# A mixer layer with a routed expert stage: one order for both sides of every condition, and last blocks of at most 64 rows with high and low parts side by side

## The chip, the cores and the metric

One core of a Trainium2 chip runs the whole kernel in one launch. The metric is the device time of one execution in microseconds (us), taken as the median of several executions. A profile is one further execution, recorded instruction by instruction.

## What is computed

One decoder layer on 2048 tokens of width 1024, in float32. First a mixer (an S5 state-space branch and a convolution branch, merged by gates, projected and normalised), then a mixture of 32 SwiGLU experts, of which each token uses two, then a second layer norm. The change touches the expert stage only; the reference of that stage, cut to what matters:

```python
zg = xt @ w_rg + b_rg                      # 4 groups: the best one is taken
ze = xt @ w_re + b_re                      # 8 experts a group: the best two of the group
gate = p_group * softmax(top_v)
eid = gsel * 8 + top_i                     # 4096 assignments of tokens to experts
# the tokens of an expert are put into blocks of ROW_BLOCK = 128 rows
def expert_block(args):
    idx, e = args
    xb = xt[idx]                                              # 128 x 1024
    hid = jax.nn.silu(xb @ w_gate[e]) * (xb @ w_up[e])        # 128 x 256
    return hid @ w_down[e]                                    # 128 x 1024
y = segment_sum(y_buf * w_buf[:, None], tok_buf, num_segments=n_tok)
```

How many rows an expert has is known only when the router has run. With the inputs of this case the counts of the 32 experts are 121, 75, 114, 74, 129, 25, 158, 106, 205, 200, 227, 36, 276, 286, 255, 177, 50, 58, 174, 160, 11, 119, 273, 99, 42, 54, 130, 211, 60, 77, 19 and 95. So 18 experts (called single here) have one block, 11 have two and 3 have three: 49 blocks. The last block has at most 64 rows in 18 experts: in nine single ones (5, 11, 16, 17, 20, 24, 25, 28 and 30) and in nine larger ones (4, 6, 12, 13, 15, 18, 19, 22 and 26).

## The kernel before

The mixer and the router take the span's first 1255 us or so; nothing of the change lies in them but a few small VectorE instructions of the router (`route2`), which turn a token's rank within its expert into a row of a table in HBM, `td`. The table says for each expert, block and partition which token stands there and with what weight. It is read back as `TAB` (`lists`).

**Arithmetic.** A product in full precision is made of three TensorE passes: each operand is split into a high part, rounded by ScalarE (ACT), and a low part, which VectorE (DVE) subtracts out; high x high, high x low and low x high are summed in PSUM. For an expert the weights are split as `egu` (gate and up, 8 pieces of 128 rows, four ACT copies and four DVE subtractions of 128x1024) and `edn` (down, two of each). A block's rows are split as `bh` and `bl` after they are transposed.

**A block.** `gateup` is 24 matmuls of 128x512 into `pg`; `act` makes `hid` from it (SiLU on ACT, a product on DVE); `turn` transposes the next block's gathered rows (eight into `pt`, from which ACT and DVE make `bh` and `bl`); `down` is 12 matmuls into `pd`, for the block before the present one, whose transposed `hid` is `hh` and `hl`; `turnh` transposes the present `hid` (two into `ph`). `emit` copies `pd` to `yy` on ACT, scaled by the rows' weights, and GpSimd (POOL) adds `yy` to the output rows in HBM by an indirect DMA, `acc`. TensorE's order is therefore `gateup`, `turn`, `down`, `turnh`, block after block. Whoever looks at a trace can take the first `ph` transpose as the mark between two blocks.

**Conditions.** The count is read into a register on each engine, and each engine branches for itself. `unit(e, b)` does a block and asks whether the expert has another; if so, it turns that block's rows and calls itself, if not, `over()` turns the next expert's rows. `JB = 4` blocks are written out for each expert, one within another, so that the ending `over()` stands four times in each expert's code, and the one of a single expert last: TensorE jumps there over three blocks and three endings, which are some 400 instructions with the weight loads. A two-block expert jumps over some 270. (An expert with more than 128 JB rows would get a loop at the end, which no expert of these inputs needs.)

**Weights.** While expert e is in its first block, `step` and `high`, `low` split the gate and up weights of expert e+1, whose raw bytes SP's queue loaded earlier, and then ask for those of e+3 (`load`); `high(1 - j, 4, 5)` and `low` do the same for `down`, once the old ones have been used.

Of the kernel before, what the change touches and what calls it, by code (L numbers as in the profile page):

```python
# [31 lines left out]
JB = 4  # L32
# [53 lines left out]
def layer(ctx, tc, a, out, dbg=None):  # L86
# [1102 lines left out]
    def route2(p, pk):  # L1189
# [7 lines left out]
        dv = oh[:, :, :, 0]  # L1197
        V.tensor_scalar(dv, rk, 1.0 / 128.0, -0.498, op0=OP.mult, op1=OP.add)
        V.scalar_tensor_tensor(rk, rk, 32.0, ef, op0=OP.mult, op1=OP.add)
        V.tensor_scalar(dv, dv, MAGIC, None, op0=OP.add)  # L1200
        V.tensor_scalar(dv, dv, MAGIC, -65535.0, op0=OP.subtract, op1=OP.mult)
        V.scalar_tensor_tensor(sl, rk, 16.0, dv, op0=OP.mult, op1=OP.add)
# [59 lines left out]
    for p in range(NP):  # L1262
# [47 lines left out]
        if p == NP - 3:  # L1310
# [30 lines left out]
    XA, XE = [[ep.tile([128, D], F32, name=f"{n}{i}") for i in range(2)] for n in ("xa", "xe")]  # L1341
    XC = [ep.tile([128, D], F32, name="xc0"),
          wp.tile([128, D], F32, name="xc1", tag="raw", bufs=1, padded_shape=[128, 1024])]
    zero = ident[:, 0:1].to_broadcast([128, D])
    for t in XA:
        A.activation(t, zero, AF.Copy, scale=0.0)
    high(0, 4, 5)
    for t in XE + XC:
        A.activation(t, zero, AF.Copy, scale=0.0)
    high(1, 0, 1)  # L1350

    def pairs(n, name, shape, dt=F32):
        return [ep.tile(shape, dt, name=f"{name}{i}") for i in range(n)]

    BH, BL = [[wp.tile([128, 8, 128], F32R, name=f"{nm}{i}", tag=tag, bufs=2) for i in range(2)]
              for nm, tag in (("bh", "hi"), ("bl", "lo"))]
    HH = pairs(2, "hh", [128, 2, 128], F32R)
    HL = pairs(2, "hl", [128, 2, 128], F32R)
    HID = pairs(2, "hid", [128, FF])
    TAB = ep.tile([128, NE, JB, 2], I32, name="tab")  # L1360
    IXL = pairs(3, "ixl", [128, 2], I32)
    IXQ = pairs(3, "ixq", [128, 2], I32)
# [3 lines left out]
    CNT, IX = {}, {}  # L1366

    def table(e):
        CNT[e] = nc.values_load(cnt[0:1, e:e + 1], engines=ENG, min_val=0, max_val=S)
        IX[e] = TAB[:, e]  # L1370
# [4 lines left out]
    def ends(e, b):  # L1375

        for t, r in ((IXL[e % 3], IX[e][:, b]), (IXQ[e % 3], IX[e][:, b - 1] if b else IXL[(e - 1) % 3])):
            V.tensor_copy(t[:, 0:1], r[:, 0:1])
            V.tensor_copy(t[:, 1:2].bitcast(F32), r[:, 1:2].bitcast(F32))
            if not e:  # L1380
                break
# [11 lines left out]
    def turn(xb, i):  # L1393
        for b in range(2):
            for k in range(4):
                PE.transpose(PT[b][:, k, :], xb[:, (4 * b + k) * 128:(4 * b + k + 1) * 128], ident)
            hi = BH[i][:, 4 * b:4 * b + 4, :]
            A.activation(hi, PT[b], AF.Copy)
            V.tensor_tensor(BL[i][:, 4 * b:4 * b + 4, :], PT[b], hi.bitcast(F32), op=OP.subtract)

    def gateup(i, gu):
        p, hi, lo = PG[i], BH[i], BL[i]
        for k in range(8):
            t = gu[k // 4]
            PE.matmul(p, hi[:, k, :], t[:, 0, k % 4, :], start=k == 0, stop=False)
            PE.matmul(p, hi[:, k, :], t[:, 1, k % 4, :], start=False, stop=False)
            PE.matmul(p, lo[:, k, :], t[:, 0, k % 4, :], start=False, stop=k == 7)

    def act(i, j):
        A.activation(HID[j], PG[i][:, 0:FF], AF.Silu)  # L1410
        V.tensor_tensor(HID[j], HID[j], PG[i][:, FF:2 * FF], op=OP.mult)

    def turnh(j):
        for k in range(2):
            PE.transpose(PH[:, k, :], HID[j][:, 128 * k:128 * k + 128], ident)
        A.activation(HH[j], PH, AF.Copy)  # L1416
        V.tensor_tensor(HL[j], PH, HH[j].bitcast(F32), op=OP.subtract)

    def down(j):
        hh, hl, dn = HH[j], HL[j], DN[j]  # L1420
        for h in range(2):
            c = slice(512 * h, 512 * h + 512)
            for k in range(2):
                PE.matmul(PD[h], hh[:, k, :], dn[:, 0, k, c], start=k == 0, stop=False)
                PE.matmul(PD[h], hh[:, k, :], dn[:, 1, k, c], start=False, stop=False)
                PE.matmul(PD[h], hl[:, k, :], dn[:, 0, k, c], start=False, stop=k == 1)

    def emit(ixc):
        y = ep.tile([128, D], F32, name="yy", bufs=2)
        for h in range(2):  # L1430
            A.activation(y[:, 512 * h:512 * h + 512], PD[h], AF.Copy, scale=ixc[:, 1:2].bitcast(F32))
        G.indirect_dma_start(out=acc, out_offset=bass.IndirectOffsetOnAxis(ap=ixc[:, 0:1], axis=0),
                             in_=y, in_offset=None, bounds_check=S - 1, oob_is_err=False, compute_op=OP.add)

    def unit(e, b):

        i, j = (e + b) % 2, e % 2
        gateup(i, GU[j])
        more = b == 0 and 0 < e < NE - 1
        if more:  # L1440
            step(1 - j, 0, 1, 2)
            high(1 - j, 3)
        if b == 1 and JB > 3:
            with tc.If(CNT[e] > 384):
                gather(XE[j], IX[e][:, 3, 0:1])
# [5 lines left out]
        jp, ixp = (j, IX[e][:, b - 1, :]) if b else (1 - j, None)  # L1451
# [10 lines left out]
        if b + 1 == JB:  # L1462
            over()
            return
        with tc.If(CNT[e] > 128 * (b + 1)) as c:
            turn((XE[j], XC[j], XE[j])[b], 1 - i)
            if e or b:
                down(jp)
                emit(ixp if b else IXL[(e - 1) % 3])
            turnh(j)  # L1470
            unit(e, b + 1)
        with c.Else():
            over()

    def extra(e):
        with tc.If(CNT[e] > 128):
            gather(XE[e % 2], IX[e][:, 1, 0:1])
            with tc.If(CNT[e] > 256):
                gather(XC[e % 2], IX[e][:, 2, 0:1])

# [4 lines left out]
    lists(2, NE - 2)  # L1485
    high(1, 2, 3, 4, 5)
    low(1, *range(6))
    for e in range(3):
        table(e)
    load(3, 1)  # L1490
    load2(3, 1)
    gather(XA[0], IX[0][:, 0, 0:1])
    gather(XA[1], IX[1][:, 0, 0:1])
    extra(0)
    turn(XA[0], 0)
    for e in range(NE):
        j = e % 2
        if e + 3 < NE:
            table(e + 3)
        if e + 2 < NE:  # L1500
            gather(XA[j], IX[e + 2][:, 0, 0:1])
        if e + 1 < NE:
            extra(e + 1)
        unit(e, 0)
        ahead_ = 0 < e < NE - 1
        if ahead_:
            high(1 - j, 4, 5)
            low(1 - j, 4)
        turnh(j)
        if ahead_:  # L1510
            low(1 - j, 5)
            if e + 3 < NE:
                load2(e + 3, 1 - j)
        if e:
            emit(IXQ[e % 3])
    down((NE - 1) % 2)
    emit(IXL[(NE - 1) % 3])
# [7 lines left out]
    with tc.If(mx > 128 * JB):  # L1525
        with tc.For_i(0, NE, 1) as e:
            c = nc.values_load(cnt[0:1, ds(e, 1)], engines=ALL, min_val=0, max_val=S)
            with tc.If(c > 128 * JB):
# [3 lines left out]
                with tc.For_i(JB, S // 128, 1) as b:  # L1532
                    with tc.If(c > b * 128):
# [3 lines left out]
                        gather(XA[0], ix[:, 0:1])  # L1537
                        turn(XA[0], 0)
                        gateup(0, GU[0])
                        act(0, 0)  # L1540
                        turnh(0)
                        down(0)
                        emit(ix)
# [133 lines left out]
```

## Time and profile before

| | us |
|---|---|
| median of 3 runs | 1860.15 (1859.89 to 1860.32) |
| the profiled execution | 1859.71 |
| its span, first to last instruction | 1857.6 |
| expert stage, first to last `ph` transpose of a block | 1285.97 to 1780.03 |

The profiled execution is 0.44 us below the median of the runs, and its time is 2.1 us more than its span. TensorE is busy for most of the span, in the mixer by nearly unbroken matmuls; in the expert stage all of TensorE, ACT, DVE and the DMA queues have work in each block, and which of them ends last differs from block to block. The granted clock of TensorE is given as a share of full speed.

### The profile page before, as it was taken

The page shows a single profiled execution, that of the slowest core. Times are in us where ns is not written, and L with a number is a line of the kernel's source. Part 1 is how long each engine was busy: PE and PEld are TensorE (multiplying, and loading weights), DVE is VectorE, ACT ScalarE, POOL GpSimd, SP SyncE. Part 2 cuts the span into 40 slices and gives each one's busy share as a digit, 9 for nine tenths or more (in the row PEclk, how much of TensorE's full clock was granted, in tenths as well). Part 3 has the DMA queues.
Part 4 walks back from the last instruction along what each step waited for, and adds up shares of the span by engine and source line. Part 5 has one row for each costly group of instructions (what it writes and reads, how often), then busy time and mean ns, then how long its engine had stood idle before and what let it go on. Part 6 is the DMA issues. An engine that isn't in the chain of part 4 may idle for free. (4 is left out here: it accounts for less than half of the span.)

```text
span 1857.6 us, 24068 instructions
## 1 busy us (share of the span) xinstructions
PE 1712.9 (92%) x8360; PEld 1376.4 (74%) x8361; DVE 1321.3 (71%) x2528; ACT 692.6 (37%) x1069; POOL 301.1 (16%) x318
## 2 busy tenths in 40 slices
PE   8999999999999999999999999974899998999940
PEld 7888877777777777877888888853677787877730
DVE  5798787687877884765576678885665556657748
ACT  5111222222222223533321122235665556657744
POOL 2000001101110110000000012212333332323215
PEclk9999999999999999999999999987999999999975
DMA  6321432432342336433553323456888878789755
GB/s 217 92 91 47 121 75 76 141 97 84 97 144 79 97 98 222 121 108 110 185 184 118 143 91 125 171 190 211 266 264 256 269 204 265 220 251 322 231 176 232
DMA packets 213924, 301.40 MB, mean 162 GB/s; under 512 B 29246, under 2 KB 159376, under 8 KB 211168
## 3 DMA queue, kind: packets, MB, share of 16 engines
q1 hardware_dynamic: 166496, 213.32, 35.4%
q0 software_dynamic: 23008, 56.06, 10.9%
q10 hardware_dynamic: 24224, 29.50, 4.7%
q8 instruction: 112, 1.84, 0.4%
q14 instruction: 84, 0.69, 0.1%
HBM read 224.28 MB, written 92.31 MB: 170 GB/s over the span
## 5 line engine op out<-in xcount | busy, mean ns | idle before, releaser
L66 PE MATMUL mm<-xh,whi 128*128 128x512 f32 x896 | 360.8, 403 | 0.0
L66 PE MATMUL mm<-xl,whi 128*128 128x512 f32 x896 | 353.5, 395 | 0.0
L66 PE MATMUL mm<-xh,wlo 128*128 128x512 f32 x896 | 352.2, 393 | 0.0
L66 DVE SCALAR_TENSOR_TENSOR cvw<-cvw,cw 128x1024 f32<-128x1024 f32 x240 | 292.1, 1280 | 0.0
L66 PE MATMUL pg<-egu,bh 128*128 128x512 f32 x784 | 251.5, 402 | 4.7 <-ACT hh L1416 2.8
L66 PEld LDWEIGHTS mm<-xh,whi 128*128 128x128 f32 x896 | 168.3, 188 | 47.9 <-ACT y L712 5.8
L66 PEld LDWEIGHTS mm<-xh,wlo 128*128 128x128 f32 x896 | 168.2, 188 | 41.4
L66 PEld LDWEIGHTS mm<-xl,whi 128*128 128x128 f32 x896 | 168.6, 188 | 36.4 <-issue 0.2
L66 DVE TENSOR_TENSOR egu<-eraw,egu 128x1024 fp32r<-128x1024 f32 x128 | 150.8, 1220 | 33.9 <-ACT egu L1245 33.9
L66 PEld LDWEIGHTS pg<-egu,bh 128*128 128x128 f32 x784 | 145.3, 190 | 37.6 <-ACT hh L1416 3.3
L66 PE MATMUL mm<-yt,whi 128*128 128x512 f32 x512 | 163.8, 401 | 2.0 <-ACT yt L858 1.5
L66 PE MATMUL mm<-wo,mh 128*128 128x512 f32 x512 | 163.6, 401 | 0.0
L66 PE MATMUL pg<-egu,bl 128*128 128x512 f32 x392 | 156.1, 398 | 1.1 <-DVE bl L66 1.1
L731 ACT ACTIVATE gt<-mm,cols 128x512 f32<-128x512 f32 x64 | 44.0, 687 | 265.5 <-PE mm L66 265.5
L66 PE MATMUL pd<-edn,hh 128*128 128x512 f32 x392 | 131.3, 416 | 11.3 <-issue 9.4
L1245 ACT ACTIVATE egu<-eraw 128x1024 fp32r<-128x1024 f32 x128 | 124.9, 1058 | 0.2 <-issue 0.2
L66 PEld LDWEIGHTS mm<-yt,whi 128*128 128x128 f32 x512 | 96.7, 190 | 26.0 <-ACT yt L858 1.5
L66 PEld LDWEIGHTS mm<-wo,mh 128*128 128x128 f32 x512 | 95.0, 190 | 21.8 <-issue 1.2
L66 DVE TENSOR_TENSOR edn<-erd,edn 128x1024 fp32r<-128x1024 f32 x64 | 77.9, 1219 | 38.8 <-ACT edn L1245 38.6
L66 PE MATMUL mm<-yt,wlo 128*128 128x512 f32 x256 | 101.7, 397 | 0.0
L66 PE MATMUL mm<-wo,ml 128*128 128x512 f32 x256 | 101.7, 397 | 0.0
L66 PEld LDWEIGHTS pd<-edn,hh 128*128 128x128 f32 x392 | 72.5, 195 | 27.4 <-issue 11.4
(287 smaller groups left out, 2646.3 us busy)
## 6 DMA issues: line engine op xcount, KB each, us to landing
eraw<-in_w_gate_dram SPq DMA_DIRECT2D x64, 512.0 KB
eraw<-in_w_up_dram SPq DMA_DIRECT2D x64, 512.0 KB
erd<-in_w_down_dram SPq DMA_DIRECT2D x32, 1024.0 KB
gd<-gt ACTq DMA_DIRECT2D x64, 256.0 KB
gl<-gd SPq DMA_DIRECT2D x64, 256.0 KB
wraw<-in_w_in_dram SPq DMA_DIRECT2D x28, 512.0 KB
xt<-in_x_dram SPq DMA_DIRECT2D x16, 512.0 KB
rg<-in_x_dram SPq DMA_DIRECT2D x8, 1024.0 KB
```

The source lines that it names most:

```text
L66: return f(*args, **kw)
L731: A.activation(gt, p, AF.Sigmoid, bias=cols[:, BI + 12 + m:BI + 13 + m])
L1245: A.activation(h, src, AF.Copy)
```

## The change

- `JB` is 3. The table `td` is laid out so that rows of a last block of at most 64 can also be read as 64 partitions (`TB2`): three more DVE instructions in each `route2`.
- `select()` works out for all experts at once, before the first block, which rows come next (`NX`) and which row list and weights a last block has (`LL`, `LQ`): some 27 small DVE instructions, and some 17 for masks ahead of it. The four small copies that `ends()` made for each expert are gone.
- `unit` and `over` give way to `block` and `further`. Both sides of the question whether there is another block end with `turnh()` alone; `turn` and `down` of the next expert stand ahead of the question, so they aren't copied. Some 272 instructions of TensorE are now jumped over by a single expert, some 137 by a two-block one.
- Each block asks whether it has more than 64 rows. If not, `gateup_small` uses `BE` as the stationary matrix: the 64 columns of the high part beside the 64 of the low part (every second column of each), so that 16 matmuls instead of 24 do; the result for the high part lies in PSUM's partitions 0 to 63, for the low part in 64 to 127. `act_small` copies the lower half out (`T`, ACT, 64x512), adds the upper half (DVE), and goes on with 64 rows.
- `B`, `HH`, `HL` and `HID` have one buffer each instead of two. The scale and the addition of an expert's last block (`emit`) come behind `turnh` of the next expert, ahead of the splitting of `edn`.

The diff, cut to its core:

```diff
-JB = 4
+JB = 3
...
-    def unit(e, b):
-
-        i, j = (e + b) % 2, e % 2
-        gateup(i, GU[j])
...
-        def over():
-            ends(e, b)
-            if e + 1 < NE:
-                turn(XA[1 - j], 1 - j)
-            if e or b:
-                down(jp)
-            if b and not e:
-                emit(ixp)
...
-        with tc.If(CNT[e] > 128 * (b + 1)) as c:
-            turn((XE[j], XC[j], XE[j])[b], 1 - i)
-            if e or b:
-                down(jp)
-                emit(ixp if b else IXL[(e - 1) % 3])
-            turnh(j)
-            unit(e, b + 1)
-        with c.Else():
-            over()
...
+    BE = B.rearrange("p k q (r t) -> p k (q r) t", t=2)[:, :, :, 0]
...
+    def gateup_small(i, gu):
+
+        p = PG[i]
+        for k in range(8):
+            t = gu[k // 4]
+            for q in range(2):
+                PE.matmul(p, BE[:, k], t[:, q, k % 4, :], start=k == 0 and q == 0, stop=k == 7 and q == 1)
+
+    def act_small(i):
+        A.activation(T, PG[i][64:128], AF.Copy)
+        V.tensor_tensor(T, T, PG[i][0:64], op=OP.add)
+        A.activation(HID[0:64], T[:, 0:FF], AF.Silu)
+        V.tensor_tensor(HID[0:64], HID[0:64], T[:, FF:2 * FF], op=OP.mult)
...
+    def block(e, b, i, gu):
+
+        with tc.If(CNT[e] > 128 * b + 64) as c:
+            gateup(i, gu)
+            act(i)
+        with c.Else():
+            gateup_small(i, gu)
+            act_small(i)
+
+    def further(e, b):
+
+        j = e % 2
+        with tc.If(CNT[e] > 128 * b) as c:
...
+            turnh()
+            block(e, b, (e + b) % 2, GU[j])
+            if e + 1 < NE or b + 1 < JB:
+                turn(XB[b])
+            down(j)
...
+        with c.Else():
+            turnh()
...
+    for e in range(NE):
+        j = e % 2
+        more = 0 < e < NE - 1
...
         if more:
             step(1 - j, 0, 1, 2)
             high(1 - j, 3)
-        act(i, j)
+        block(e, 0, j, GU[j])
         if more:
             low(1 - j, 3)
...
+        turn(XN[j])
+        if e:
+            down(1 - j)
+        further(e, 1)
+        if e:
+            emit(LQ[:, e, 0:1], LQ[:, e, 1:2])
+        if more:
             high(1 - j, 4, 5)
-            low(1 - j, 4)
-        turnh(j)
+            low(1 - j, 4, 5)
...
```

**ACT, at the change from one expert to the next.** Before, the splitting of the down weights stands ahead of the copy of the turned `hid`:

```order
L1245 ACTIVATE edn_10194<-erd 128x1024 x2
L1416 ACTIVATE hh_10166<-ph 128x256
L1431 ACTIVATE yy<-pd_10181,ixq_10177 128x512
L1431 ACTIVATE yy<-pd_10182,ixq_10177 128x512
L1369 TENSOR_LOAD cnt
L1476 COMPARE_AND_BRANCH
L1478 COMPARE_AND_BRANCH
L1478 UNCONDITIONAL_BRANCH x2
L1476 UNCONDITIONAL_BRANCH
L1245 ACTIVATE egu_9529<-eraw_9327 128x1024 x2
L1245 ACTIVATE egu_9995<-eraw_9327 128x1024 x2
L1410 ACTIVATE hid_10171<-pg_10180 128x256
```

In the changed program the same place of ACT reads:

```order
L1488 ACTIVATE hh<-ph 128x256
L1522 UNCONDITIONAL_BRANCH
L1503 ACTIVATE yy<-pd_10219,lq 128x512
L1503 ACTIVATE yy<-pd_10220,lq 128x512
L1249 ACTIVATE edn_10173<-erd 128x1024 x2
L1439 TENSOR_LOAD cnt
L1564 COMPARE_AND_BRANCH
L1567 COMPARE_AND_BRANCH
L1567 UNCONDITIONAL_BRANCH x2
L1564 UNCONDITIONAL_BRANCH
L1249 ACTIVATE egu_10179<-eraw_9816 128x1024 x2
L1249 ACTIVATE egu_10233<-eraw_9816 128x1024 x2
```

The two copies of `edn` have moved from ahead of `hh` to behind the two `yy`.

**DVE, in an expert's first block.** Before, DVE goes from the weights to `hid` and `bl` in this order (behind the branch are the rows of an expert with a further block):

```order
L66 TENSOR_TENSOR egu_9529<-eraw_9327,egu_9529 128x1024 x2
L66 TENSOR_TENSOR egu_9995<-eraw_9327,egu_9995 128x1024
L66 TENSOR_TENSOR hid_10171<-hid_10171,pg_10180 128x256
L66 TENSOR_TENSOR egu_9995<-eraw_9327,egu_9995 128x1024
L1465 COMPARE_AND_BRANCH
L66 TENSOR_TENSOR bl_10164<-pt_10183,bh_10162 128x512
L66 TENSOR_TENSOR bl_10164<-pt_10184,bh_10162 128x512
```

In the changed program there are two ways through the question on 64 rows:

```order
L66 TENSOR_TENSOR egu_9544<-eraw_9339,egu_9544 128x1024 x2
L66 TENSOR_TENSOR egu_10013<-eraw_9339,egu_10013 128x1024
L1512 COMPARE_AND_BRANCH
L66 TENSOR_TENSOR hid<-hid,pg_10218 128x256
L1512 UNCONDITIONAL_BRANCH
L66 TENSOR_TENSOR tt<-tt,pg_10218 64x512
L66 TENSOR_TENSOR hid<-hid,tt 64x256
L1512 UNCONDITIONAL_BRANCH
L66 TENSOR_TENSOR egu_10013<-eraw_9339,egu_10013 128x1024
```

The addition `tt` of a small block stands behind three subtractions of the next expert's weights, as `hid` does, and the fourth subtraction is still ahead of the low part of the rows.

**TensorE, in an expert's first block.** The changed program has the gate and up products twice, of which one is run:

```order
L66 MATMUL pg_10217<-egu_9544,bhl 128x512 x12
L66 MATMUL pg_10217<-egu_10013,bhl 128x512 x12
L1512 UNCONDITIONAL_BRANCH
L66 MATMUL pg_10217<-egu_9544,bhl 128x512 x8
L66 MATMUL pg_10217<-egu_10013,bhl 128x512 x8
L1512 UNCONDITIONAL_BRANCH
L66 MATMUL pt_10221<-ident,xhi 128x128 x4
```

Before, the end of that block, at the question whether there is another, was this:

```order
L66 MATMUL pg_10180<-egu_10191,bh_10163 128x512 x2
L66 MATMUL pg_10180<-egu_10191,bl_10165 128x512
L1465 COMPARE_AND_BRANCH
L66 MATMUL pt_10183<-ident,xe_10147 128x128 x4
L66 MATMUL pt_10184<-ident,xe_10147 128x128 x4
L66 MATMUL pd_10181<-edn_10152,hh_10166 128x512 x2
```

The `pt` rows now follow the products on every way; before, they stood on each side of the branch `L1465`, and a single expert's stood behind all others.

## Rows read from the trace of the kernel before

**Rows 1.** Windows: length, busy (instructions) of PE, PEld, DVE, ACT, POOL; clock; DMA.
```profile
1500.00:1550.00 50.00, 50.00 (x247) 41.09 (x246) 26.39 (x47) 27.75 (x45) 13.22 (x8) 1.00 0.75 209
```

**Rows 2.** Groups by line, PE, 1280 to 1790: busy, mean, idle before, releaser.
```profile
L66 PE MATMUL pg<-egu,bh 128*128 128x512 f32 x781 | 250.0, 401 | 4.7 <-ACT hh L1416 2.8 <-ACT edn L1245 1.7
L66 PE MATMUL pd<-edn,hh 128*128 128x512 f32 x392 | 131.3, 416 | 11.3 <-issue 9.4 <-ACT yy L1431 1.9
L66 PE MATMUL pt<-ident,xa 128*128 128x128 f32 x248 | 32.9, 275 | 9.4 <-issue 8.9 <-DMA xa<-hd,tab 0.5
L66 PE MATMUL ph<-ident,hid 128*128 128x128 f32 x98 | 19.0, 276 | 1.6 <-DVE ixl L66 1.4
```

**Rows 3.** Timeline of PE: start, length, instruction; expert 23's block, and the ends.
```profile
1285.97 0.41 PE L66 MATMUL ph<-ident,hid 128*128 128x128 f32 x2
...
1668.76 0.38 PE L66 MATMUL ph<-ident,hid 128*128 128x128 f32 x2
...
1669.44 0.39 PE L66 MATMUL pg<-egu,bl 128*128 128x512 f32 x1
...
1674.55 1.03 PE L66 MATMUL pt<-ident,xa 128*128 128x128 f32 x8
1675.34 0.72 PE L66 MATMUL pd<-edn,hh 128*128 128x512 f32 x2
...
1678.23 0.38 PE L66 MATMUL ph<-ident,hid 128*128 128x128 f32 x2
...
1780.03 0.38 PE L66 MATMUL ph<-ident,hid 128*128 128x128 f32 x2
```

**Rows 4.** Waits of PE for nothing shown, 1280 to 1790: total us, times, longest.
```profile
PE pd L66 <- issue: 9.8, 5, 4.7
PE pt L66 <- issue: 8.9, 7, 2.8
```

**Rows 5.** Timeline of PE, first waits behind the jumps of experts 3 and 17.
```profile
1315.18 1.07 PE L66 MATMUL pt<-ident,xa 128*128 128x128 f32 x8 [2.52 <-issue]
...
1573.27 1.22 PE L66 MATMUL pd<-edn,hh 128*128 128x512 f32 x2 [4.74 <-issue]
```

**Rows 6.** Windows, as rows 1, the six microseconds at that wait.
```profile
1572.00:1578.00 6.00, 4.73 (x15) 3.78 (x16) 1.59 (x7) 0.87 (x1) 0.00 (x0) 0.72 1.06 357
```

**Rows 7.** Timeline of ACT, expert 23's block.
```profile
1668.26 2.01 ACT L1245 ACTIVATE edn<-erd 128x1024 fp32r<-128x1024 f32 x2 [1.41 <-PE pd L66]
1670.17 0.36 ACT L1416 ACTIVATE hh<-ph 128x256 fp32r<-128x256 f32 x1
1670.43 1.25 ACT L1431 ACTIVATE yy<-pd,ixq 128x512 f32<-128x512 f32 x2
1671.58 3.90 ACT L1245 ACTIVATE egu<-eraw 128x1024 fp32r<-128x1024 f32 x4
```

**Rows 8.** Timeline of DVE, expert 23's block.
```profile
1672.67 3.50 DVE L66 TENSOR_TENSOR egu<-eraw,egu 128x1024 fp32r<-128x1024 f32 x3 [0.55 <-ACT egu L1245]
1676.08 0.41 DVE L66 TENSOR_TENSOR hid<-hid,pg 128x256 f32<-128x256 f32 x1
1676.41 1.22 DVE L66 TENSOR_TENSOR egu<-eraw,egu 128x1024 fp32r<-128x1024 f32 x1
1677.55 0.21 DVE L66 COPY ixl<-tab 128x1 int32<-128x1 int32 x2
1677.79 1.28 DVE L66 TENSOR_TENSOR bl<-pt,bh 128x512 fp32r<-128x512 f32 x2
```

**Rows 9.** Waits, 1280 to 1790: total us, times, longest.
```profile
ACT yy L1431 <- DMA acc<-yy,ixq: 13.7, 9, 2.8
```

**Rows 10.** Timelines of POOL, PE and DVE at the first block.
```profile
1268.21 1.90 POOL L1384 DMA_INDIRECT xa<-hd,tab  x1 [7.28 <-ACT egu L1245]
...
1276.33 1.94 PE L66 MATMUL pt<-ident,xa 128*128 128x128 f32 x8 [21.68 <-DMA xa<-hd,tab]
...
1278.08 0.69 DVE L66 TENSOR_TENSOR bl<-pt,bh 128x512 fp32r<-128x512 f32 x1 [6.64 <-ACT bh L1398]
```

More of the change, by code (lines that the diff above doesn't have):

```diff
@@ L1340, in layer, with rowt @@
     ep = ex.enter_context(tc.tile_pool(name="ep", bufs=1, side="right"))
-    XA, XE = [[ep.tile([128, D], F32, name=f"{n}{i}") for i in range(2)] for n in ("xa", "xe")]
-    XC = [ep.tile([128, D], F32, name="xc0"),
-          wp.tile([128, D], F32, name="xc1", tag="raw", bufs=1, padded_shape=[128, 1024])]
+    def rowt(tag):
+        return wp.tile([128, D], F32, name=f"x{tag}", tag=tag, bufs=2, padded_shape=[128, 1024])
+    X1, X2 = rowt("hi"), rowt("lo")
+    XN = [rowt("hi"), rowt("lo")]
@@ L1344, in layer @@
+    XB = [None, X1, X2]
     zero = ident[:, 0:1].to_broadcast([128, D])
-    for t in XA:
-        A.activation(t, zero, AF.Copy, scale=0.0)
+    A.activation(X1, zero, AF.Copy, scale=0.0)
     high(0, 4, 5)
-    for t in XE + XC:
+    for t in XN + [X2]:
         A.activation(t, zero, AF.Copy, scale=0.0)
     high(1, 0, 1)
[L1352 to L1356, printed above, removed]
@@ L1364, in layer @@
+    NX = ep.tile([128, NE, JB], I32, name="nx")
+    LP = ep.tile([128, NE, JB, 2], F32, name="lp")
+    LL = ep.tile([128, NE, 2], I32, name="ll")
+    LQ = ep.tile([128, NE, 2], I32, name="lq")
     ENG = [ET.PE, ET.Activation, ET.DVE, ET.Pool]
     ALL = ENG + [ET.SP]
-    CNT, IX = {}, {}
+    CNT = {}
+    for b in range(JB):
+        V.tensor_scalar(MK[:, :, b], pc, 128.0 * b, None, op0=OP.is_gt)
+    V.memset(MK[:, :, 0:1], 1.0)
+    V.tensor_tensor(OH[:, :, 0:JB - 1], MK[:, :, 0:JB - 1], MK[:, :, 1:JB], op=OP.subtract)
@@ L1368, in table @@
     def table(e):
         CNT[e] = nc.values_load(cnt[0:1, e:e + 1], engines=ENG, min_val=0, max_val=S)
-        IX[e] = TAB[:, e]
-    def lists(e, n):
-        A.dma_start(TAB[:, e:e + n].rearrange("p e b c -> p e (b c)"), dap(td, 32 * e, [[1024, 128], [32, n], [1, 2 * JB]]))
[L1375 to L1381, printed above, removed]
@@ L1403, in gateup @@
         for k in range(8):
             t = gu[k // 4]
[L1405 to L1413, printed above, removed]
+            PE.matmul(p, B[:, k, 0], t[:, 0, k % 4, :], start=k == 0, stop=False)
@@ new lines, in layer @@
+    low(0, 4, 5)
+    load2(2, 0)
+    lists(0, 2)
+    lists(2, NE - 2)
+    A.dma_start(TB2.rearrange("p e b c -> p e (b c)"), dap(td, 0, [[2048, 64], [32, NE], [1, 2 * JB]]))
+    gather(X1, TAB[:, 0, 0, 0:1])
+    high(1, 2, 3, 4, 5)
+    low(1, *range(6))
+    for e in range(2):
+        table(e)
+    load(3, 1)
+    load2(3, 1)
+    select()
+    gather(XN[0], NX[:, 0, 0:1])
+    turn(X1)
+    for e in range(NE):
+        j = e % 2
+        more = 0 < e < NE - 1
+        if e + 2 < NE:
+            table(e + 2)
+        if e + 1 < NE:
+            gather(XN[1 - j], NX[:, e + 1, 0:1])
+        with tc.If(CNT[e] > 128):
+            gather(X1, NX[:, e, 1:2])
+            if JB > 2:
+                with tc.If(CNT[e] > 256):
+                    gather(X2, NX[:, e, 2:3])
```

172 lines of the change are left out of this document (100 added, 72 removed).

## The prediction

> **What bounds the kernel now.** I read the windows of the expert stage first, then TensorE's groups there, and last the timelines of one block. TensorE's share of the whole span is an average over a mixer that the change leaves alone and the expert stage, and only the latter decides. There a stretch without disturbance has TensorE busy 50.00 of 50 us at full clock [rows 1], and one with a disturbance 4.73 of 6 us at 0.72 [rows 6]. So most blocks are bound by TensorE and a few are disturbed.
>
> The undisturbed block is that of expert 23: from one `ph` to the next 9.47 us (1668.76 to 1678.23) [rows 3]. From the `bl` matmul at 1669.44 to the transposes at 1674.55 lie 22 matmuls in 5.11 us, 0.232 each; the transposes take 0.79 and `down` with its hand-over 2.89. The 48 periods between the 49 marks last 494.06 us (1285.97 to 1780.03); at 9.47 they would last 454.6. So 39.5 us are lost. TensorE's own groups name 27.0 us of idle time, of which 18.3 us are "issue", that is, waits for nothing that the profile shows, ahead of `pt` or `pd` matmuls [rows 2]: twelve waits, up to 4.7 us long [rows 4]. These stand just behind a jump out of an expert's code: 2.52 us at expert 3, 4.74 us at expert 17 [rows 5], and the six microseconds around the latter have the clock at 0.72 and the DMA engines full (1.06) [rows 6]. The rest of the 39.5 us, some 12, is the slower clock behind these pauses. I put 27 us down to the jumps: the 18.3, and 1.7 us (six microseconds at 0.72) about five times over.
>
> The other engines are close behind TensorE in a single expert's block. ACT has per block `edn` 1.91, `hh` 0.26, `yy` 1.15 (by the starts of the rows that follow), `egu` 3.8 (four of half an `edn`) [rows 7], and `hid` and `bh`, an estimated 1.3 by the sizes of `hh` and `yy`: 8.4 of 9.47. DVE has six pieces of 1.14 us (three in 3.41), `hid`, `hl` and `bl`, and its order is a chain: three `egu`, `hid`, the fourth `egu`, `bl` at 1677.79, that is 9.03 after the mark, so its first half is there at 9.7; TensorE needs it with its third matmul, 0.68 behind the next mark, at 10.15 [rows 3, 8]. The slack is 0.5 us.
>
> **The change, part by part.** The sum is made against the profiled execution, 1859.71 us, 0.44 below the median.
>
> (1) Sixteen matmuls for 24 in nine last blocks of larger experts: 8 x 0.232 = 1.86 each [rows 3], in all -16.7. There no weights are split, and the longer way to `hid` (copy 0.58 as one `yy`, addition 0.6 as one half of `bl`, SiLU and product some 0.7, hand-overs 0.6: 2.5 us) [rows 7, 8] is covered by `turn` and `down`, 3.68. No row shows a weight load whose columns lie two apart. Below, it costs nothing more; above, if it took twice its time and set the pace, the 16 would take about as long as 24 and the -16.7 be gone. I take nothing, since the row nearest to it is this kernel's own undisturbed matmul, 0.232 us, under which each load is hidden.
>
> (2) The same in nine single experts. Here TensorE's 1.86 us are worth nothing, because ACT and DVE become the bound. From the mark, T0: `hh` at 0.5, `yy` to 1.9, `edn` to 3.8, `egu` to 7.6, copy of the lower half to 8.2. DVE: the first `edn` piece at 2.9, five pieces of 1.14 to 8.6, addition to 9.2; SiLU on ACT to 9.6, product to 9.95, next mark at about 10.2. That is 0.7 more than 9.47. The fourth `egu` then ends at 11.1 and the first half of `bl` at 11.7, when TensorE wants it at 10.9: 0.8 more, in the next block. Some 1.6 each, +15. Below: 0, if the copy gets ahead; above: 2.4 each, 22.
>
> (3) First blocks of more than 64 rows. `edn` on ACT and DVE starts behind `hh` and `yy` instead of half a microsecond ahead of the mark, so DVE's five pieces end at 8.6 instead of 7.3, `hid` at 8.95, `egu` at 10.1, the first half of `bl` at 10.7, against 10.15 [rows 3, 7, 8]. That is 0.55 in the next block. Where that next block is again a single expert's, its own chain starts at the mark and the delay has given it time, so the loss comes in every second one: 14 of 21 such experts, +7.5. Below 0, above 12.
>
> (4) The jumps. Before, the jumps over some 400 instructions (single) and 270 (two blocks) cost 27 us together. In the changed program a single expert jumps as far as a two-block one did, and a two-block one over half of that. By jump length alone, 27 us over the 29 experts with such a jump are 0.93 each, which with 18 jumps of 272 gives 17 left; if short jumps cost nothing, 0 is left. I take 9: -18, between the two ends, nearer to neither. [...]
>
> (5) `ends()` goes, four copies on DVE. The 0.24 us that they took ahead of `bl` [rows 8] is counted in (3); the one wait for them ahead of a `ph`, 1.4 us [rows 2], goes: -1.4.
>
> (6) `yy`. ACT waited 13.7 us in nine places for an earlier addition to have read `yy` [rows 9], mostly hidden. Emits per expert's code are three instead of four, so that the two buffers alternate from single to single; with two-block experts they now meet the same one again. Its cost is now behind `hh`, where the splitting of the weights follows. +2, between 0 and 10.
>
> (7) TensorE's pauses in (2) are up to 2.6 us a block and may bring the clock down as the pause of 4.74 did [rows 5, 6]; where TensorE is not the bound that is free, in the block after it not: +3, between 0 and 8.
>
> (8) The start. `route2`: three small instructions, two times in the open, 1 us. `select()`, some 27 small instructions of some 0.15 us, 4 us, lies in the 6.64 us in which DVE waits for the first `bh` [rows 10]; but the gather of expert 1's rows now waits for it. The first gather took 8.1 us from its issue at 1268.21 to the transposes at 1276.33 [rows 10], so one issued at 1275.5 is there at 1283.6, when `turn` wants it. +1.5 in all, between 0.5 and 6.
>
> Sum: -16.7 + 15 + 7.5 - 18 - 1.4 + 2 + 3 + 1.5 = -7.1, so 1852.6, said as 1852. [...]
>
> **The rivals.** Slower: the jumps cost what they cost (instructions are still fetched from the same full queues [rows 6], now at two more branches a block). Then (4) is 0 and the time 1870. For it: the waits stand at full DMA queues, which the change leaves full. Against: there is less code to skip. It decides from 11 us staying beyond my 9.
>
> Faster by more: the waits of (2) and (3) don't come, because ACT gets to `edn` sooner than I reckon, and all 18 small blocks gain. Then (2) and (3) are 0, and the time is 1830. For it: half a microsecond of slack and my chain's hand-overs are rough. Against: DVE's pieces stand in the order that I added up.
>
> Slower as well: the load at a step of two takes twice its time. Then (1) is gone and single blocks lose too: 1870 to 1875.
>
> Also slower: expert 1's rows, or those of others, come late because the gathers are asked for later; at 8 us from issue to use [rows 10] one lateness in each of ten experts by 1.5 us gives 1867.
>
> Faster by (4) alone: no jump of 272 instructions or fewer waits. Then the 9 that I left are 0, and the time is 1844. For it: twelve waits in 29 experts leave most jumps without one [rows 4]; against: nothing in the rows tells the lengths apart. [...]
>
> **How the numbers follow.** Within 0.2%, 1856.4 to 1863.9, a measurement of this kernel can't tell from no change. Forecast, 1845 to 1861: 0.40, of which 0.13 is "same". No waits of ACT and DVE, 1822 to 1845: 0.23. No jump waits, 1840 to 1848: 0.08. Jumps cost as before, 1865 to 1874: 0.17. Slow load: 0.07. Late gathers: 0.05. Faster 0.27 + 0.23 + 0.08 = 0.58, same 0.13, slower 0.29. The range leaves out the lower half of the second case and the upper ends: 1832 to 1870.
>
> **What would show it.** Right: extra blocks of at most 64 rows with a period near 7.6; single ones near 10.2, with ACT and DVE named ahead of `ph`, and `bl` ahead of `pg` after them; "issue" waits of TensorE of some 6 us in place of 18.3. Wrong: a matmul of the small kind longer than 0.24 us from start to start (slow load); "issue" waits as before; single small blocks at 9.4 or below (no ACT/DVE bound); a `pt` that waits for its gather.

## The result, and the profile after

The changed kernel takes 1875.53 us (1873.0 to 1876.2, four runs) against 1860.24 for the kernel before in the same comparison: ratio 1.0083, 95% interval 1.007 to 1.0096. It is slower, by some 15 us; the forecast was 1852, and the upper end of its range, 1870, is missed by 5.5. The profiled execution took 1873.0, the lowest of the four and 2.5 below their median; its span is 1871.1.

The first mark of the expert stage stands at 1293.17, 7.2 us later than in [rows 3], and the last at 1794.10: the 48 periods last 500.9 us instead of 494.1. So half of the loss is the start, and the other half is what is left over in the blocks when large gains and large losses are set off. TensorE's groups of the changed kernel, 1280 to 1810 (columns as in [rows 2]), show both:

```profile
L66 PE MATMUL pg<-egu,bhl 128*128 128x512 f32 x1030 | 268.1, 418 | 47.6 <-DVE hl L66 29.8 <-DVE bhl L66 8.7 <-ACT yy L1503 5.1
L66 PE MATMUL pd<-edn,hh 128*128 128x512 f32 x392 | 126.7, 404 | 1.3 <-ACT yy L1503 1.3
...
L66 PE MATMUL pt<-ident,xhi 128*128 128x128 f32 x240 | 31.1, 273 | 1.2 <-issue 0.9 <-DMA xhi<-hd,nx 0.3
...
L66 PE MATMUL ph<-ident,hid 128*128 128x128 f32 x98 | 19.3, 278 | 14.0 <-DVE hid L66 14.0
```

The waits ahead of `pd` and `pt` that came to 20.7 us in [rows 2] are down to 2.5. The wait ahead of `pg` has grown from 4.7 (with 1.1 more on the `bl` matmuls) to 47.6 us, and that ahead of `ph` from 1.6 to 14.0. The instruction that ends most of the former is `hl`. That is odd: `hl` is the low part of `hid`, which the gate matmuls don't read. The timeline of TensorE at experts 22 to 25 shows where it stands (a row's idle time and what ended it stand in brackets):

```profile
1666.55 0.38 PE L66 MATMUL ph<-ident,hid 128*128 128x128 f32 x2
...
1674.16 0.38 PE L66 MATMUL ph<-ident,hid 128*128 128x128 f32 x2
1674.45 5.75 PE L66 MATMUL pg<-egu,bhl 128*128 128x512 f32 x24
...
1683.71 0.38 PE L66 MATMUL ph<-ident,hid 128*128 128x128 f32 x2
1686.10 3.96 PE L66 MATMUL pg<-egu,bhl 128*128 128x512 f32 x16 [2.01 <-DVE hl L66]
1689.91 1.03 PE L66 MATMUL pt<-ident,xhi 128*128 128x128 f32 x8
...
1694.34 0.41 PE L66 MATMUL ph<-ident,hid 128*128 128x128 f32 x2 [0.63 <-DVE hid L66]
1697.00 5.53 PE L66 MATMUL pg<-egu,bhl 128*128 128x512 f32 x16 [2.26 <-DVE hl L66]
```

A further block of at most 64 rows has the period 7.61 that was forecast (1666.55 to 1674.16), and its 16 matmuls go in 3.81 us (1686.10 to 1689.91), 0.238 each, against 0.232 in expert 23's block (22 in 5.11 us) [rows 3], so the loads at a step of two are not slow. But behind a single expert's block TensorE stands still for 2 us, and the 16 matmuls behind the second such pause take 5.53 us instead of 3.96; the granted clock was 0.65 between 1697 and 1701. DVE in the same stretch:

```profile
1683.21 1.21 DVE L66 TENSOR_TENSOR egu<-eraw,egu 128x1024 fp32r<-128x1024 f32 x1
1684.35 1.27 DVE L66 TENSOR_TENSOR bhl<-pt,bhl 128x512 fp32r<-128x512 f32 x2
1685.55 0.41 DVE L66 TENSOR_TENSOR hl<-ph,hh 128x256 fp32r<-128x256 f32 x1
```

The first half of `bhl` is there about 1684.95 and the second about 1685.6; the gate starts at 1686.10, when `hl` has ended. In expert 1's block the same is seen with more room:

```profile
1304.17 1.28 DVE L66 TENSOR_TENSOR bhl<-pt,bhl 128x512 fp32r<-128x512 f32 x2
1305.63 0.39 PE L66 MATMUL ph<-ident,hid 128*128 128x128 f32 x2
1306.68 0.42 DVE L66 TENSOR_TENSOR hl<-ph,hh 128x256 fp32r<-128x256 f32 x1 [1.22 <-ACT hh L1488]
1307.25 5.78 PE L66 MATMUL pg<-egu,bhl 128*128 128x512 f32 x24 [1.23 <-DVE hl L66]
```

There the low part of the rows was ready ahead of the mark at 1305.63, and the gate still started only at 1307.25, behind `hl`. The program suggests a reason, which the run `a_first` below tests: the waits are for a count of finished instructions, not for one instruction. The rows of the next block, `bhl`, are written ahead of the question and again on its long side, so the gate behind the question would wait for the count that they have on the long side. On the short side nothing but `turnh` stands, so that its one ACT and one DVE instruction, `hh` and `hl`, would have to add the counts of all that was skipped. By that the gate waits for `hh` (3.7 us in all) and `hl` (29.8) on the short side, although it doesn't use them.

The start, in the timelines of ACT, DVE and TensorE:

```profile
1263.32 7.43 ACTq L1546 DMA_DIRECT2D tab<-td  x1
1270.79 2.00 ACT L1249 ACTIVATE egu<-eraw 128x1024 fp32r<-128x1024 f32 x2 [8.30 <-issue]
...
1271.88 2.36 DVE L66 TENSOR_TENSOR egu<-eraw,egu 128x1024 fp32r<-128x1024 f32 x2 [8.15 <-ACT egu L1249]
...
1276.43 0.20 DVE L66 CAST tf<-tab 128x96 f32<-128x96 int32 x1
...
1281.88 1.28 DVE L66 TENSOR_TENSOR bhl<-pt,bhl 128x512 fp32r<-128x512 f32 x2
...
1282.62 8.11 PE L66 MATMUL pg<-egu,bhl 128*128 128x512 f32 x22 [5.49 <-DVE bhl L66]
1290.82 1.28 ACT L1468 ACT_TABLE_LOAD   x1 [14.12 <-PE pg L66]
```

The issue of the extra list `TB2` held ACT's queue for 7.43 us, so the last weight pieces came later on ACT and DVE, `select()` started at 1276.43 instead of in DVE's idle time of [rows 10], and 5.4 us of it stood ahead of the first low part. TensorE, whose rows had been turned 2 us earlier than before, waited 5.49 us, and its 22 matmuls then took 8.11 us; the granted clock was 0.50 from 1284 to 1288, against 1.00 from 1289 to 1290. Of the 7.2 us at the mark, 3.5 lie ahead of these matmuls, 2.3 in them and 1.4 behind them. For the last there is a cause that the prediction doesn't have: the table load of ACT's SiLU, 1.28 us, ran while the gate was under way before (at 1278.92), and now stands behind the gate, so that the mark waits 1.58 us for `hid`.

### The profile page after: what moved, and what is told of

Same layout as the page of the kernel before. It is cut to its first block, busy times and chain, and to the rows that moved or that the text cites. A ratio compares the mean times of both kernels' runs of the same rounds, so it can differ in the third digit from the quotient of the medians.

```text
span 1871.1 us, 24098 instructions
## 1 busy us (share of the span) xinstructions
PE 1691.8 (90%) x8224; PEld 1356.1 (72%) x8225; DVE 1335.2 (71%) x2490; ACT 707.3 (38%) x1088; POOL 312.7 (17%) x319
## 4 chain that ended last, share of the span: by engine, by line
PE 72%; issue 10%; DMA 9%; DVE 8%; ACT 1%; POOL 0%; another core or an unknown queue 0%; DVEq 0%; POOLq 0%; ACTq 0%; SPq 0%
PE mm L66 51%; PE pg L66 8%; PE aux L66 7%; PE pd L66 4%; DMA acc<-yy,lq 3%; DMA td<-r_sd,r_sl 2%; DMA acc<-yy,ll 2%; DVE f L66 1%; DVE egu L66 1%; PE pt L66 1%; DMA xhi<-hd,nx 1%; DVE cvw L66 1%; DVE f_q L66 1%; DVE edn L66 1%; DMA xt<-in_x_dram 1%
## 5 line engine op out<-in xcount | busy, mean ns | idle before, releaser
L66 PE MATMUL pg<-egu,bhl 128*128 128x512 f32 x1032 | 269.4, 418 | 47.6 <-DVE hl L66 29.8
L66 DVE SCALAR_TENSOR_TENSOR cvw<-cvw,cw 128x1024 f32<-128x1024 f32 x240 | 292.1, 1280 | 0.0
L66 PEld LDWEIGHTS pg<-egu,bhl 128*128 128x128 f32 x1032 | 203.6, 202 | 101.2 <-ACT yy L1503 25.3
L66 PE MATMUL pd<-edn,hh 128*128 128x512 f32 x392 | 126.7, 404 | 1.3 <-ACT yy L1503 1.3
L1504 POOL DMA_INDIRECT acc<-yy,lq x31 | 49.3, 1589 | 258.7 <-ACT yy L1503 258.7
L1210 POOL DMA_INDIRECT td<-r_sd,r_sl x32 | 37.7, 1179 | 312.5 <-DVE r_sl L66 303.6
```

The costliest lines, as they stand in the source:

```text
L66: return f(*args, **kw)
L1210: d = G.indirect_dma_start(out=td, out_offset=bass.IndirectOffsetOnAxis(ap=sl[:, t, k:k + 1], axis=0), in_=sd[:, t, k, :], in_offset=None)
```

## The experiments

Differences below are of medians; where two versions were not measured side by side, a span from the difference of their ratios to that of the medians is given. The changed kernel's ratio is 1.0083.

**One `turnh` behind the question** (`a_join`).

```diff
...
-            else:
-                turnh()
-        with c.Else():
-            turnh()
...
         further(e, 1)
+        turnh()
...
```

Expected: 

> The changed kernel with turnh once, behind the question whether there is another block, in place of one on each side of it. Theory J: the first gate matmul of the next expert waits 1.2 to 2.3 us in nearly every expert because, on the short side, the counts of all skipped instructions are added by that side's only ACT and DVE instruction, hh and hl; with turnh outside they are added before it. Then TensorE's idle time ahead of pg falls from 47.6 us to 10 to 20 (what is left is named bhl), the single big experts' period from 10.9 to 9.5 to 10, and the time to 1845 to 1860. Rival D, the chain of the prediction: DVE is simply late with the low part of the rows; then pg waits stay above 35 us with another name, and the time above 1868.

Measured: 1900.03 us, ratio 1.0206 (1.0181 to 1.0231), slower by 23 to 25 us than the changed kernel. Neither expectation holds as a whole: rival D has the time, but the waits ahead of `pg` are 32.3 us, below its 35. TensorE's waits, total, times and longest:

```profile
PE ph L66 <- DVEq L1522: 44.4, 19, 6.3
PE pg L66 <- ACT hh L1488: 16.6, 19, 1.1
PE pg L66 <- DVE bhl L66: 6.7, 5, 3.7
```

The wait for `hl` is gone from `pg`, but its twin stands ahead of `ph`: the releaser is no working instruction of DVE but its sequencer at the question (`DVEq L1522`). By the same reading of the program, `hid` too is written ahead of the question and again on its long side, so that `turnh` behind the question waits until DVE has come to the question's end, which is behind the fourth `egu` and both `bhl`; measured are the 44.4 us in 19 places under that name. Theory J had the mechanism and missed its second victim.

**The same, with `edn` ahead of `turnh`** (`a_join_edn`).

```diff
+        if more:
+            high(1 - j, 4, 5)
+            low(1 - j, 4)
         turnh()
+        if more:
+            low(1 - j, 5)
...
-            high(1 - j, 4, 5)
-            low(1 - j, 4, 5)
...
```

Expected: 

> The same, and the splitting of the down weights ahead of turnh again, as before the change. If the later start of edn is what fills ACT and DVE in the first blocks (part 3 of the prediction), the low part of the rows is there 1.3 us earlier: pg waits below 8 us, 5 to 15 us less than the version with turnh outside alone. If it is not (DVE has time enough once the skipped counts no longer hold TensorE), the two are within 3 us of each other.

Measured: 1873.12 us, ratio 1.007 (1.0047 to 1.0092), 27 us less than `a_join`, more than the 5 to 15 expected; that wait of `ph` fell from 44.4 to 20.7 us, and the `pg` waits, expected below 8, stayed where they were (32.2). Where the end of DVE's chain is waited for, the place of `edn` is worth far more than I had given it.

**The extra list on another queue, half of `select()` later** (`a_select`).

```diff
...
-    A.dma_start(TB2.rearrange("p e b c -> p e (b c)"), dap(td, 0, [[2048, 64], [32, NE], [1, 2 * JB]]))
...
+    SP.dma_start(TB2.rearrange("p e b c -> p e (b c)"), dap(td, 0, [[2048, 64], [32, NE], [1, 2 * JB]]))
     select()
     gather(XN[0], NX[:, 0, 0:1])
     turn(X1)
+    select2()
...
```

Expected: 

> The changed kernel with the extra list TB2 asked for by SP's queue behind its weight loads, not by ACT's, and with the part of select() that makes the last blocks' lists behind the first block's turn. Theory S: the first mark came 7.2 us later because ACT was held 8.3 us by the issue of that list, DVE with it, and then 5.4 us of select() stood ahead of the first low part. Then the first mark goes from 1293.2 to 1284 to 1288 and the time down by 5 to 9 us, to 1866 to 1871. Rival: the first gather or the slower clock sets the start; then the mark moves by less than 2 us and the time stays.

Measured: 1868.71 us, ratio 1.0036 (1.0016 to 1.0056): 7 to 9 us less than the changed kernel, as expected. The first mark moved by 3.7 us only, to 1289.44 and not to 1284 to 1288:

```profile
1277.84 1.94 PE L66 MATMUL pt<-ident,xhi 128*128 128x128 f32 x8 [23.46 <-DMA xhi<-hd,tab]
1289.44 0.41 PE L66 MATMUL ph<-ident,hid 128*128 128x128 f32 x2 [1.58 <-DVE hid L66]
```

The first gather now lands last, at 1277.84, later than in either kernel. The wait of 1.58 us for `hid` behind the table load is still there. In the two profiled executions the 3.7 us at the mark are all that was won (the 48 periods last 502.2 us and 500.9); where the rest came from is not shown, and the intervals leave room for it to be chance.

**The jumps as long as before** (`a_jb4`): `JB = 4`, so that single experts jump over 410 instructions and two-block ones over 272.

```diff
-JB = 3
+JB = 4
...
-    XB = [None, X1, X2]
+    XB = [None, X1, X2, X1]
...
+            if b > 2:
+                gather(X1, NX[:, e, 3:4])
```

Expected: 

> The changed kernel with JB = 4, so that single experts jump over 410 instructions of TensorE and two-block ones over 272, as before the change. Theory F: the jumps' length made the waits named issue. Then these come back (10 to 20 us on pt, pd or ph in place of 0.9), partly under the gate's wait, and the time is 1882 to 1895. Rival H: the waits went because the jump now comes behind down, where TensorE waits for hl anyway; then issue waits stay below 3 us and the time within 4 us of 1875.

Measured: 1901.93 us, ratio 1.0214 (1.019 to 1.0237): 24 to 26 us slower than the changed kernel, and above the expected range. The profiled execution, at 1911.44 us, is the slowest of the five. TensorE's waits in it:

```profile
PE pg L66 <- DVE hl L66: 34.5, 25, 2.3
PE ph L66 <- issue: 18.7, 7, 3.6
PE pg L66 <- ACT egu L1249: 5.8, 1, 5.8
```

The waits for nothing shown are back, 18.7 us as against 9.8 and 8.9 in [rows 4], now ahead of `ph`, since the jump now stands there; all seven are behind single experts. The 5.8 us behind expert 3's jump are named after a splitting of the next expert's weights, which this gate doesn't read; they may be of the same kind, which is not shown. Theory F holds, though the price is above what it gave; rival H falls.

**Something else to carry the counts** (`a_first`): one 1x1 instruction on ACT and one on DVE at the head of the short side.

```diff
...
+    def first():
+        A.activation(DA, ident[0:1, 0:1], AF.Copy)
+        V.memset(DV, 0.0)
...
         with c.Else():
+            first()
             turnh()
...
```

Expected: 

> The changed kernel with one tiny instruction more on ACT and on DVE (1x1) ahead of turnh on the short side of the question. Theory J: the short side's first instruction carries the counts of all that is skipped, so these two take them over from hh and hl, and the gate no longer waits for hl, nor turnh for the join. Then hl, hh and yy vanish as what pg waits for (38 us in the changed kernel), pg waits are 5 to 20 us named bhl or the small instruction, ph waits 10 to 20 for hid, and the time 1850 to 1864. Rival D: DVE is late anyway; pg waits stay above 35 us and the time above 1870.

Measured: 1866.65 us, ratio 1.0047 (1.0031 to 1.0062), 7 to 9 us less than the changed kernel, a little short of the expected range. The waits:

```profile
PE ph L66 <- DVE hid L66: 20.3, 9, 4.2
PE pg L66 <- DVE dv L66: 11.6, 10, 1.9
PE pg L66 <- ACT yy L1505: 10.4, 7, 1.9
PE pg L66 <- DVE bhl L66: 7.2, 8, 1.5
```

With two instructions of no use added and nothing taken away, `hl` is gone from the list, the gate now waits for `dv`, which it doesn't read any more than `hl`, and the `pg` waits fell from 47.6 to 30.2 us: so the wait was one for a count and not for data. Behind expert 1's block, where the gate waited 1.23 us in the rows above, it doesn't wait at all in `a_first`. Rival D is half right, though: 20.3 us of `ph` waits (14.0 before) and the 7.2 for `bhl` say that DVE and ACT really are late as well. `dv` stands right behind the second half of `bhl`, so that most of its 11.6 us is lateness too.

**The same, with `edn` ahead of `turnh` on both sides** (`a_first_edn`).

```diff
+    def ending(e):
+        more = 0 < e < NE - 1
+        if more:
+            high(1 - e % 2, 4, 5)
+            low(1 - e % 2, 4)
+        turnh()
...
             first()
-            turnh()
+            ending(e)
...
```

Expected: 

> The same, with edn (both ACT copies and the first DVE subtraction) ahead of turnh on both sides, as it stood before the change. If the later edn is what delays the low part (part 3 of the prediction), this gives 5 to 20 us back against a_first; if hh now waits behind edn and that counts, it loses up to 5.

Measured: 1854.12 us, ratio 0.9978 (0.9967 to 0.9988); 12.5 us less than `a_first`, measured beside it. `ph` waits for `hid` fell from 20.3 to 8.1 us:

```profile
PE ph L66 <- DVE hid L66: 8.1, 8, 2.8
```

**The start as well** (`a_all`): the edit of `a_select` on top.

Expected: 

> The same, with the list TB2 on SP's queue and the second part of select() behind the first turn, as in a_select, where that gave 6.8 us. The gains should add: 5 to 8 us below a_first_edn.

Measured: 1850.27 us, ratio 0.9952 (0.9937 to 0.9967); 3.9 us less, a little under what was expected. So without the false wait, with the early `edn` and with the start mended the changed kernel is 24 to 25 us faster. That this is near the forecast of 1852 is chance, since the forecast held 9 us for the last two.

**First blocks always in 24 matmuls** (`a_all_big`).

```diff
-        block(e, 0, j, GU[j])
+        gateup(j, GU[j])
+        act(j)
...
-    for b in range(JB):
+    for b in range(1, JB):
         V.tensor_scalar(NM, pc, 128.0 * b + 64.0, None, op0=OP.is_le)
```

Expected: 

> The same, with all first blocks in 24 matmuls, the nine small single ones too; only further blocks of at most 64 rows keep the 16. If part 2 of the prediction holds (ACT and DVE bind there, with one more copy and one more addition), this is 5 to 15 us faster than a_all; if TensorE's 1.86 us are worth something in single blocks, it is up to 15 us slower.

Measured: 1837.93 us, ratio 0.9894 (0.9878 to 0.9911): 12.3 us less than `a_all`. The single small blocks lost time by taking fewer matmuls. The edit also takes the question on 64 rows out of all other first blocks; but in the two profiled executions the 48 periods are 15.6 us shorter together, and 13.2 of these lie in the nine small single blocks and the blocks right behind them. TensorE's waits, 1280 to 1830:

```profile
PE pt L66 <- DMA xhi<-hd,nx: 4.5, 5, 1.9
PE pt L66 <- issue: 3.8, 3, 2.1
PE pg L66 <- ACT egu L1249: 3.5, 1, 3.5
PE pg L66 <- ACT yy L1507: 2.7, 1, 2.7
PE ph L66 <- DVE hid L66: 2.1, 2, 1.5
```

The 3.5 and the 2.7 us stand ahead of a gate behind the jumps of two single experts (11 and 24), and name ACT instructions that this gate doesn't read. In three more such places it waits 1.1 to 2.0 us. They may be waits behind jumps under another name; no run shows it.

**The same in the changed kernel** (`a_big`): that edit alone.

Expected: 

> The changed kernel with all first blocks in 24 matmuls, the nine small single ones too, and nothing else. In a_all_big against a_all that gave 12.3 us. If it is a cost of the small path itself (one more copy and addition on engines that are full), it gives 8 to 14 us here too, 1861 to 1868, and the ph waits for hid (14.0 us) go; if the wait for hl takes its place, less than 5.

Measured: 1866.66 us, ratio 1.0047 (1.0031 to 1.0064): 7 to 9 us less than the changed kernel. `ph` waits for `hid` fell from 14.0 to 2.8 us; the wait for `hl` fell from 29.8 only to 19.6:

```profile
PE ph L66 <- DVE hid L66: 2.8, 3, 1.5
PE pg L66 <- DVE hl L66: 19.6, 13, 2.3
```

The nine small single blocks themselves last as long as before (101.5 and 101.9 us together); what is won is won in the blocks right behind them (114.4 and 109.8).

**The late `edn` in the kernel before** (`b_order`): `turnh` and `emit` ahead of the splitting of `edn`, nothing else.

```diff
+        turnh(j)
+        if e:
+            emit(IXQ[e % 3])
         if ahead_:
             high(1 - j, 4, 5)
-            low(1 - j, 4)
-        turnh(j)
-        if ahead_:
-            low(1 - j, 5)
+            low(1 - j, 4, 5)
...
```

Expected: 

> The kernel before with one thing of the change: the splitting of edn behind turnh and emit, not ahead of them. If the order of ACT's work costs by itself what a_first_edn gave back against a_first (12.5 us), this is 8 to 15 us slower than the kernel before, with bl or a DVE instruction named ahead of ph or pg. If it costs only together with the waits at the join, it is within 4 us of it.

Measured: 1878.46 us, ratio 1.0107 (1.0088 to 1.0126): 20.5 us slower than the kernel before, more than expected. The waits:

```profile
PE pt L66 <- issue: 9.5, 7, 2.5
PE pd L66 <- issue: 9.4, 5, 5.0
PE pg L66 <- ACT hh L1416: 6.4, 8, 1.0
PE ph L66 <- DVE ixl L66: 6.1, 10, 0.8
PE pg L66 <- DVE bl L66: 5.1, 9, 0.6
```

The jumps' waits are as in [rows 4]; new are short waits, ten ahead of `ph` and nineteen ahead of `pg`. So this one order costs more than the whole change did. But only 5.1 us bear the name of the low part, `bl`. The wait ahead of `ph` is again one for a count, as at expert 5:

```profile
1354.38 0.41 DVE L66 TENSOR_TENSOR hid<-hid,pg 128x256 f32<-128x256 f32 x1
1355.85 0.20 DVE L66 COPY ixl<-tab 128x1 int32<-128x1 int32 x2
1356.05 0.44 PE L66 MATMUL ph<-ident,hid 128*128 128x128 f32 x2 [0.70 <-DVE ixl L66]
```

`hid` had ended 1.3 us earlier, and `ph` doesn't read `ixl`: that is one of the copies of `ends()`, the first DVE instructions on the short side of the old question. The kernel before has this wait too, once (1.4 us in [rows 2]). So `b_order` doesn't separate the order from the waits at the question's end.

**No 16-matmul blocks at all** (`a_all_24`): `block` is `gateup` and `act` in every block of `a_all_big`.

Expected: 

> As a_all_big, but every block in 24 matmuls: the 16 are gone altogether. Part 1 of the prediction says that the nine further small blocks are worth 16.7 us where TensorE binds: then this is 1850 to 1856. By the periods of a_all_big (7.6 us where nothing waits, but 8.66 on the mean of the nine) they are worth 0.8 us each: then 1842 to 1847. If the branch on 64 rows costs more than the 16 matmuls give, it is at or below 1838.

Measured: 1840.44 us, ratio 0.99 (0.9883 to 0.9917), not to be told from `a_all_big`, and below both expected ranges. From first to last mark it took 469.25 us (1292.22 to 1761.47), `a_all_big` 469.41 (1289.46 to 1758.87); 2.8 us lie between their first marks, and 1.4 of these in the wait for the first gather (25.8 and 24.4 us). In the best version the 16 matmuls are worth nothing that can be measured. Yet the nine further small blocks are 14.6 us longer without them (92.5 and 77.9 us together). That is won back elsewhere: 13.2 us of it in the nine small single blocks and the blocks right behind them, whose code is the same in both versions. The edit changes one thing more: without the second copy of the products a single expert's jump is shorter by some 64 instructions (an estimate: 16 matmuls and as many loads in each of two blocks), and the gates behind such jumps wait 4.3 us in all, instead of 12.4. So the price of the 16 may be the longer jump; the two were not separated.

## Why the prediction was wrong, by its own steps

**What failed: a wait that it doesn't have.** It has no term for the new shape of the question, and asked of waits only which data is late. The questions on 64 rows stand in the sum at nothing too, and no run shows what they cost alone: `a_all_24`, which has none of them and no 16 matmuls, took 1840.44 us, and `a_all_big`, which has both in further blocks, 1837.93. Ending both sides with `turnh` alone made the gate wait for the short side's last ACT and DVE instructions. In the changed kernel 38.6 us of the idle time ahead of `pg` bear the names `hl`, `yy` and `hh` (29.8, 5.1 and 3.7); taking the count off `hl` gave 7 to 9 us (`a_first`). Most of the rest is real lateness that shows once the false wait is gone. The old question had waits of this kind as well, but there the copies of `ends()` and the rows of `turn` stood on the short side ahead of `hl` and carried the counts; the prediction counted the end of `ends()` as a gain (5), and took the carriers away with it. This last is read from the program and from `a_first`, which puts two carriers back; no run has `ends()` back alone.

The sum missed by 23 us. The false wait, the late `edn` and the start, taken away one after the other, bring 24 to 25 us (`a_all`), and stood in the sum with 9; so some 15 of the 23 lie in them, and the rest in the parts below, which partly cancel and aren't measured one by one.

**(3), the late `edn`, was mis-sized.** Predicted +7.5, bounds 0 and 12; measured +20.5 alone in the kernel before (`b_order`) and 12.5 given back in `a_first_edn`. The mechanism was right in part. I let the delay hit every second first block, with 0.55 us. In `b_order` nine second blocks of larger experts wait 0.4 to 0.6 us for `bl`, as reckoned, and last some 0.9 longer on the mean. But eight single experts' blocks also last 10.3 to 10.5 us instead of 9.4 to 9.8, and each ends with a wait of `ph` for `ixl`, which is one for a count. How much of the 20.5 us the order would cost without them is not shown.

**(8), the start, was mis-sized.** Predicted +1.5, at most 6; measured 7.2 at the first mark. I counted `select()` into DVE's idle time and asked nothing of the queue that issues the extra list: the issue alone held ACT 7.43 us, and DVE's idle time had moved ahead of `select()`, which took 5.4 us and not 4. The clock of 0.50 behind the pause and the table load of 1.28 us in the open were not in the sum.

**(4), the jumps, had the right mechanism and too little size, the other way.** Predicted -18; `issue` waits ahead of `pt` and `pd` fell from 18.3 to 0.9 us, and making the jumps long again costs 24 to 26 us (`a_jb4`). So nearly all of the 27 us went. The length alone doesn't decide it: of the waits before, 11.6 us stood behind single experts' jumps, and 6.9 behind five two-block experts' jumps of 270 (the longest 2.83 us at 1337.05, expert 4), while the single experts' 272 now hardly wait under that name. Why is not shown.

**(2), small single blocks, was right in kind and too large.** Predicted +15 in all over a period of 9.47; with 24 matmuls in their place the kernel gains 7 to 9 us (`a_big`) or 12.3 (`a_all_big`): the blocks are bound by ACT and DVE, and the addition (0.68 us) and its copy (0.60) lengthen that; `ph` waits 14.0 us for `hid` in the changed kernel and 2.8 in `a_big`. The trace has the mark at 10.63 (1683.71 to 1694.34) where I had 10.2, with `hid` named ahead of `ph`; 2.01 us of this period are the gate's wait for `hl`. I had put half of the loss into the block itself; by `a_big` it lies in the next one.

**(1), small further blocks, was right in the block and wrong in the sum.** Where nothing else waits the period is 7.6, as forecast; in the nine it is 8.07 on the mean, 1.4 us less than 9.47 and not 1.86. By `a_all_24` the time isn't lost in the next block: it is gone from the sum where single experts' blocks follow, perhaps by the longer jumps that the second copy of the products makes, which the prediction doesn't price.

**(6) and (7).** ACT's wait for an addition to have read `yy` fell from 13.7 us to 5.6, so that nothing shows the +2. The clock I had at +3: behind the longer pauses six gates take 7.2 to 8.4 us for 24 matmuls instead of 5.6, and two take 5.4 and 5.5 for 16 instead of 3.8, with the granted clock at 0.58 from 1295 to 1298, for one; that is an estimate of 12 once the one such gate of the kernel before is taken off. The pauses are longer than I had them because the false wait is in them.

Of the rivals none came true: "jumps cost what they cost" (1870) and the slow load (1870 to 1875) gave times near the measured one for reasons that the trace refutes (0.9 us of `issue` waits ahead of `pt` and `pd`, and 0.238 us a matmul), and the count at the end of the short side was not among them. As to the fetching of instructions that the first of them speaks of: from 1280 to 1790 the kernel before has 117 packets (1.48 MB) on two DMA queues of the kind `instruction`, the changed kernel from 1280 to 1800 97 (1.22 MB); what their fetching cost is not shown.

## What to carry to other kernels

When code on two sides of a run-time question is made alike, look not only at which work is doubled but at which instruction of the short side carries the counts of the skipped ones, and who waits for a count beyond the question: here one idle instruction on each of ACT and DVE at its head took 7 to 9 us off the time (`a_first`), and work that is taken off the short side may have been doing just that. A saving on one engine is time only where nothing else is nearly full; here the chain of ACT and DVE had an estimated 0.5 us to spare in 9.47 [rows 3, 7, 8], and a third fewer gate matmuls in nine single blocks made the kernel slower, while the place of two ACT copies was worth 12 to 20 us. The shape with the shorter jumps, all blocks of full size where the weights are split, `edn` early, the two idle instructions and the extra list off ACT's queue is 1.1% faster than the kernel before.

## What the runs showed of the hardware that was not expected

The issue of a list of 48 KB in 2048 short pieces by ACT's queue lasted 7.43 us, while those of 6 and 90 KB ahead of it, in 256 and 3840 pieces of the same 24 bytes, took 0.94 together; issued by SP's queue later, the list of 48 KB took 0.70 (1269.43 in `a_select`). So the number of pieces isn't the reason; what made the difference is open. Waits of TensorE for nothing shown came to 18.7 us both in the kernel before, behind jumps of some 400 and of 270 instructions, and in `a_jb4`, behind jumps of 410 alone; in the changed kernel, with jumps of 272 and 137, they were 0.9 ahead of `pt` and `pd` and 0.3 ahead of `pg`. Behind the longest of the kernel before, of 4.74 us, the granted clock was 0.50 from 1574 to 1576.
